# Retention's entry: the first chunk's small tiles in other places, PSUM banks laid out earlier, gate matmuls ahead of the first scores, odd feature tiles first

## The chip, the core and the metric

The kernel runs on one core of a Trainium2 chip. The metric is the device time of one execution in microseconds (us); for the kernel before it is the median of three runs. Engines are named as in the profile: PE is TensorE (matmuls; PEld its weight loads), DVE is VectorE, ACT is ScalarE, POOL is GpSimd, SP is SyncE, whose queue issues most of the transfers. Names of tiles in the profile are those of the program, with buffer numbers left out.

## The reference

One decoder block in float32 on a sequence of 1024 tokens with 1024 features. The input is normalised and modulated to `h`; from `h`, three kinds of mixing run side by side (chunkwise retention, dilated attention, and gates that merge them), then comes an MLP. What the edited place computes is the retention branch, for 4 heads with keys of 256, values of 512, in chunks of 128 tokens:

```python
def step(state, inp):
    qi, ki, vi = inp
    s = jnp.einsum('bhid,bhjd->bhij', qi, ki) * inner_decay[None]
    o = (jnp.einsum('bhij,bhje->bhie', s, vi)
         + jnp.einsum('bhid,bhde->bhie', qi, state) * q_decay[None, :, :, None])
    state = (state * chunk_decay[None, :, None, None]
             + jnp.einsum('bhjd,bhje->bhde', ki * k_decay[None, :, :, None], vi))
    return state, o
...
ret_out = (jax.nn.silu(rg) * ro) @ w_ret_out
```

Here `ro` is `o` normalised over the features of its head, and `rg` is a product of `h` with a gate weight, `h @ w_in` in the columns of the retention gate.

## The kernel before, in words

The instructions of all engines stand in the order in which the program writes them; nothing reorders them afterwards. A wait is put in by the tile pools: an instruction that writes a tile waits until whoever used that memory before is done, and with `reuse_waits="tile"` this is worked out for each old tile whose memory the new one covers.

Products are made in three matmuls (`mm3`, L197 to L205): each operand is split into a high and a low part, and low times high, high times low and high times high are summed in a PSUM bank. L201, L203 and L205 in the profile are those three, for every product that goes through `mm3`.

The stage ahead of the edited place is `values` (L1182). It makes the values of all heads and chunks in seven block products for each pair of heads, on sums `vc`, `va` and others in PSUM. `v_post` (L1152 to L1180) finishes each: VectorE adds a sum into `vr` (L1176), ScalarE takes its high part (L1177), VectorE its low part (L1178), and SP stores it to DRAM (`vd<-vr`, L1180). The last four such blocks are the last work of the stage. The tiles of that stage lie in `xpool` (L330). While the last product runs, GpSimd's queue loads the second halves of the even feature tiles of `h` back from DRAM (`hh<-h12d`, `hl<-h12d`, L1211 and L1212), since the even tiles (`hh[0]`, `hh[2]`, `hh[4]`, `hh[6]` and their low parts `hl`) held sums of blocks there. The odd ones hold `h` throughout.

At its end `values` closes `xpool` and opens the retention pool in the same memory (`open_ret`, L514: first `state`, then its high and low parts `stateh`, `statel`). Then it issues the loads for the second and third chunk (`fetch`, L583; the first chunk's values, and the queries and keys of the first two, were loaded earlier), then the first chunk's scores (`s_kt(0)`, L616), and then lays the PSUM banks out anew (`banks(False)`, L148): eight single banks before, and after it four single ones and two pairs, the pairs for the gates.

`s_kt` makes the scores `sT` of a chunk (L624, L626) and the transposed keys `kT` (L631) on TensorE. ScalarE copies the scores into `sm` (L635), VectorE adds the other part (L636) and multiplies by the decay (L637), ScalarE and VectorE split the result into `smh` and `sml` (L638, L639), and the keys, with their decay, into `kh` (L645) and `kl` (L646).

Then the retention loop runs over 4 heads and 8 chunks (`chunk`, L672). For the first chunk of all (`g == 0`) it issues four of the eight feature tiles of the gate product `rg` (six matmuls each, two halves of the tokens times three parts), then `kv` from `kh`, `kl` and the values (six matmuls), copies of `kv` into `state` on VectorE (L696), the modulation sum that rides along (L452), the next chunk's scores (`s_kt(1)`), and the output `o` from `smh`, `sml` and the values (three matmuls). In later chunks `kv` stands first, then two feature tiles of the gate product, then the next scores, `o`, and the other two feature tiles. A gate product spans two chunks: feature tiles 0 to 3 in the even chunk and 4 to 7 in the odd one, in that order.

Of the kernel before, what the change touches and what calls it, by code (L numbers as in the profile page):

```python
# [11 lines left out]
F32 = mybir.dt.float32  # L12
F32R = mybir.dt.float32r
# [4 lines left out]
P = 128  # L18
D = 1024
S = 1024  # L20
NK = D // P
H = 4
C = 128
# [111 lines left out]
def block_kernel(ctx, tc, io, stop=None, dbg=None):  # L135
# [61 lines left out]
    def mm3(outs, w, xs, first, last, skip=False):  # L197

        wh, wl = w
        for o, (xh, xl) in zip(outs, xs):  # L200
            nc.tensor.matmul(o, wl, xh, start=first, stop=False, skip_group_check=skip)  # L201
        for o, (xh, xl) in zip(outs, xs):
            nc.tensor.matmul(o, wh, xl, start=False, stop=False, skip_group_check=skip)  # L203
        for o, (xh, xl) in zip(outs, xs):
            nc.tensor.matmul(o, wh, xh, start=False, stop=last, skip_group_check=skip)  # L205

    def wk(w, k):

        return w[0][:, k * P:(k + 1) * P], w[1][:, k * P:(k + 1) * P]
# [112 lines left out]
    def halves(h, l):  # L322
        return [(h[:, :512], l[:, :512]), (h[:, 512:], l[:, 512:])]

    hx = [halves(hh[k], hl[k]) for k in range(NK)]
# [149 lines left out]
        nc.vector.scalar_tensor_tensor(hl[k], xt[k], mods[:, SH1 + k:SH1 + k + 1], fv(hh[k]),  # L475
                                       op0=ALU.add, op1=ALU.subtract)

    def proj_mm(ps, w, ks=range(NK)):
        outs = ps if isinstance(ps, list) else [ps[:, 0, :], ps[:, 1, :]]
        for k in ks:  # L480
            mm3(outs, wk(w, k), hx[k], k == 0, k == NK - 1)

    def proj_gen(ps, w):
        for k in range(NK):
# [27 lines left out]
    R = {}  # L512

    def open_ret():  # L514
        x_ctx.close()
        R["p"] = ret_ctx.enter_context(tc.tile_pool(name="ret", bufs=1, reuse_waits="tile"))
        R["state"] = R["p"].tile([P, 2, DV], F32, name="state")
        R["sh"] = R["p"].tile([P, 2, DV], F32R, name="stateh")
        R["sl"] = R["p"].tile([P, 2, DV], F32R, name="statel")

    def etile(name, dt=F32):
        return R["p"].tile([P, 1024], dt, tag="E", bufs=12, name=name)
# [55 lines left out]
    hd = {}  # L578
# [37 lines left out]
    def s_kt(i):  # L616

        p = R["p"]
        g = i
        h, c = divmod(g, NC)  # L620
        t = hd["j", g]
        ps = ps_s(f"sT{h}{c}")
        for i in range(2):
            nc.tensor.matmul(ps[:, :2 * C], t[:, 0, 2 + i, :], t[:, :, i, :], start=i == 0, stop=False,  # L624
                             skip_group_check=True)
            nc.tensor.matmul(ps[:, :C], t[:, 1, 2 + i, :], t[:, 0, i, :], start=False, stop=i == 1,  # L626
                             skip_group_check=True)
        pk = ps_s(f"kT{h}{c}", (P, 2, P)) if c < NC - 1 else None
        if pk is not None:
            for i in range(2):  # L630
                nc.tensor.transpose(pk[:, i, :], hd["qk", g][:, 2 + i], ident)  # L631
        sm = p.tile([P, C], F32, tag="sm", bufs=1, name=f"sm{h}{c}")
        smh = p.tile([P, C], F32R, tag="smh", bufs=2, name=f"smh{h}{c}")
        sml = p.tile([P, C], F32R, tag="sml", bufs=2, name=f"sml{h}{c}")
        nc.scalar.copy(sm, ps[:, :C])  # L635
        nc.vector.tensor_add(sm, sm, ps[:, C:2 * C])  # L636
        nc.vector.tensor_mul(sm, sm, decay[:, h * C:(h + 1) * C])  # L637
        nc.scalar.copy(smh, sm)  # L638
        nc.vector.tensor_sub(sml, sm, fv(smh))  # L639
        hd["s", g] = (smh, sml)  # L640
        if pk is not None:
            kd = ct[:, CS_KDEC + h:CS_KDEC + h + 1]
            kh = p.tile([P, 2, P], F32R, tag="kh", bufs=1, name=f"kh{h}{c}")
            kl = p.tile([P, 2, P], F32R, tag="kl", bufs=1, name=f"kl{h}{c}")
            nc.scalar.mul(kh, pk, kd)  # L645
            nc.vector.scalar_tensor_tensor(flat(kl), flat(pk), kd, fv(flat(kh)), op0=ALU.mult, op1=ALU.subtract)  # L646
            hd["k", g] = (kh, kl)
# [24 lines left out]
    def chunk(h, c, ahead, w=None):  # L672
        p = R["p"]
        g = NC * h + c
        if g + 3 < NG:
            fetch(g + 3)
        if c % 2 == 0:
            hd["rgw"] = w
            hd["rgp"] = ps_mm(f"rg{h}{c}")
        ks = range(4 * (c % 2), 4 * (c % 2) + 4)  # L680
        if g == 0:
            proj_mm(hd["rgp"], hd["rgw"], ks)
        vh, vl = hd["v", g][:, 0], hd["v", g][:, 1]
        st, sh, sl = R["state"], R["sh"], R["sl"]
        kvs = []
        if c < NC - 1:
            kh, kl = hd["k", g]
            for i in range(2):
                kv = ps_s(f"kv{h}{c}{i}")
                mm3([kv], (kh[:, i, :], kl[:, i, :]), [(vh, vl)], True, True)  # L690
                kvs.append(kv)
        if g > 0:
            proj_mm(hd["rgp"], hd["rgw"], ks[:2])
        for i, kv in enumerate(kvs):
            if c == 0:
                nc.vector.tensor_copy(st[:, i, :], kv)  # L696
            else:
                nc.vector.scalar_tensor_tensor(st[:, i, :], st[:, i, :], float(GAMMA[h] ** C), kv,
                                               op0=ALU.mult, op1=ALU.add)
        ahead(2)  # L700
        if g + 1 < NG:
            s_kt(g + 1)
        po = ps_s(f"o{h}{c}")
        if c > 0:
            t = hd["j", g]
            for i in range(2):
                mm3([po], (t[:, 0, i, :], t[:, 1, i, :]), [(sh[:, i, :], sl[:, i, :])], i == 0, False)
        mm3([po], hd["s", g], [(vh, vl)], c == 0, True)
        if c < NC - 1:
            for i in range(2):  # L710
                nc.scalar.copy(sh[:, i, :], st[:, i, :])
                nc.vector.tensor_sub(sl[:, i, :], st[:, i, :], fv(sh[:, i, :]))
        if g + 2 < NG:
            jit_qk(g + 2)
        if g > 0:
            on_T(*divmod(g - 1, NC))
        if g > 0:
            proj_mm(hd["rgp"], hd["rgw"], ks[2:])
        bn = p.tile([P, 6], F32, tag="bn", bufs=2, name=f"bn{h}{c}")
        ba = p.tile([P, 2], F32, tag="ba", bufs=2, name=f"ba{h}{c}")  # L720
        gr = p.tile([P, 1], F32, tag="gr", bufs=2, name=f"gr{h}{c}")
        nc.vector.bn_stats(bn, po)
        nc.vector.bn_aggr(ba, bn)
        nc.vector.tensor_scalar(gr, ba[:, 1:2], ct[:, CS_QD2 + h:CS_QD2 + h + 1], GN_EPS, op0=ALU.mult, op1=ALU.add)
        nc.gpsimd.tensor_tensor(gr, gr, mhalf[:, 0:1], op=ALU.pow)
        nc.vector.tensor_mul(gr, gr, ct[:, CS_QD + h:CS_QD + h + 1])
        on = p.tile([P, DV], F32, tag="on", bufs=1, name=f"onm{h}{c}")
        nc.vector.tensor_scalar(on, po, ba[:, 0:1], gr, op0=ALU.subtract, op1=ALU.mult)
        hd["o", h, c] = on
        if c % 2 == 1:  # L730
            hd["srg", h, c // 2] = etile(f"srg{h}{c // 2}")
            nc.scalar.activation(hd["srg", h, c // 2], flat(hd["rgp"]), AF.Silu)
        if h > 0 and c < 4:
            u_final(h - 1, (c,))
# [447 lines left out]
    def values(ahead):  # L1182
        last = len(VSEQ) - 1
        for j in range(2):
            v_low(0, j)
        for i, (hp, n) in enumerate(VSEQ):
            if i + 2 <= last:
                v_load(i + 2)
            for p in range(4):
                v_mm(i, p)  # L1190
                if V["post"]:
                    v_post(*V["post"].pop())
                V["post"].append((i, p))
                if p < 2 and i < last:
                    v_w(i + 1, p)
                    if p:
                        v_low(i + 1, 0)
                if p == 2 and i < last:
                    v_low(i + 1, 1)

                if i == last - 2 and p == 2:
                    fetch(0)
                if i == last - 2 and p == 3:
                    first["release"]()
                if i == last - 1 and p in (1, 2):
                    jit_qk(p - 1)
                if i == last - 1 and p == 3:
                    ahead(2)
                if i == last and p == 0:
                    for m in range(4):  # L1210
                        nc.gpsimd.dma_start(hh[2 * m][:, 512:], h12_d[m][:, 0])  # L1211
                        nc.gpsimd.dma_start(hl[2 * m][:, 512:], h12_d[m][:, 1])  # L1212
        v_post(*V["post"].pop())
        open_ret()
        for g in (1, 2):
            fetch(g)
        s_kt(0)
        banks(False)

    for kk in range(4):  # L1220
# [1349 lines left out]
```

## Time and profile before

| | us |
|---|---|
| median of three runs | 2232.41 |
| lowest, highest of them | 2231.76, 2233.54 |
| the profiled execution, its own time | 2231.9 |
| its span, first to last instruction | 2230.1 |
| ScalarE, VectorE, GpSimd busy in the span | 912.4, 1470.1, 155.1 |

The page gives each engine's busy time, the groups of instructions that cost most, and the chain of work that ended last, followed back from the last instruction. A row of the timeline has the start and the length in us, the engine, the line, the operation, the tiles written and read, their shapes and the count; in brackets stands the idle time of the engine before it and what ended it. SPq is the queue of SP, from which transfers are issued. A matmul's length in the profile overlaps the next one's, so the pitch from start to start tells its rate.

### The profile page before, as it was taken

Reading aid. Unit: us, or ns where it says so; the run is one execution under the profiler, and the core shown is the slowest. Engines: PE = TensorE matmul, PEld = TensorE weight load, DVE = VectorE, ACT = ScalarE, POOL = GpSimd, SP = SyncE. Lnnn points to the kernel's source line nnn. Section 1 sums busy time; section 2 is a strip of 40 time slices with the busy share of each in tenths; the row PEclk is TensorE's granted clock in tenths of the full one; section 3 lists DMA queues with packets and bytes.
Section 4 is the critical chain, followed back from the end, with each engine's and each line's share of the span. In section 5 each row is a group of like instructions: output and inputs, shape, how many; then the busy total and the mean of one; then the engine's idle time right before and its main releaser. Section 6 shows DMA issues by size and latency. Waiting matters only on the chain.

```text
span 2230.1 us, 27097 instructions
## 1 busy us (share of the span) xinstructions
PE 2168.7 (97%) x10082; PEld 1796.1 (81%) x10082; DVE 1470.1 (66%) x2303; ACT 912.4 (41%) x1671; POOL 155.1 (7%) x176
## 2 busy tenths in 40 slices
PE   7999999999989999999999999999999999999998
PEld 5888888878868888888788788888778888788887
DVE  6756777754448778865555654676866665787845
ACT  4532233223324444544634633524444445533412
POOL 0100111000012112200000000002000000000003
PEclk9999999999999999999999999999999999999999
DMA  9869999634675556559723265654234444745322
GB/s 383 220 208 299 294 296 277 189 131 174 224 255 170 181 178 203 185 175 238 224 73 96 92 219 187 237 180 159 69 135 147 155 156 165 261 141 170 123 85 76
DMA packets 157602, 414.15 MB, mean 186 GB/s; under 512 B 27222, under 2 KB 55133, under 8 KB 153054
## 3 DMA queue, kind: packets, MB, share of 16 engines
q1 hardware_dynamic: 149598, 364.19, 46.5%
q0 software_dynamic: 7872, 48.24, 9.5%
q8 instruction: 79, 1.29, 0.2%
q14 instruction: 53, 0.43, 0.1%
HBM read 321.51 MB, written 156.13 MB: 214 GB/s over the span
## 4 chain that ended last, share of the span: by engine, by line
PE 86%; DVE 6%; DMA 4%; ACT 3%; issue 1%; POOL 0%; SPq 0%; POOLq 0%; DVEq 0%; ACTq 0%
PE qap L203 5%; PE qap L201 5%; PE qap L205 5%; PE fp L201 4%; PE fp L203 4%; PE fp L205 4%; PE rg L201 3%; PE rg L203 3%; PE rg L205 3%; PE f2a L203 2%; PE f2a L205 2%; PE f2a L201 2%; PE ak L201 2%; PE ak L203 2%; PE ak L205 2%; PE va L203 1%
## 5 line engine op out<-in xcount | busy, mean ns | idle before, releaser
L201 PE MATMUL qap<-hh,qaw 128*128 128x512 f32 x216 | 84.1, 390 | 0.4 <-DVE qat L285 0.4
L205 PE MATMUL qap<-hh,qaw 128*128 128x512 f32 x216 | 84.0, 389 | 0.0
L203 PE MATMUL qap<-hl,qaw 128*128 128x512 f32 x216 | 84.0, 389 | 0.0
L613 POOL TENSOR_TENSOR j<-qk,j 128x512 fp32r<-128x512 f32 x32 | 43.3, 1353 | 462.2 <-ACT j L612 462.2
L2029 ACT ACTIVATE a<-a 128x512 f32<-128x512 f32 x48 | 30.3, 632 | 79.5 <-DVE a L2028 79.5
L1926 POOL TENSOR_TENSOR accnf<-accnf,sqnf 128x256 f32<-128x256 f32 (+1 forms) x18 | 16.6, 921 | 620.2 <-ACT sqnf L1925 620.2
L1383 ACT ACTIVATE P<-P,ng 128x128 f32<-128x128 f32 (+1 forms) x96 | 41.9, 438 | 39.0 <-DVE ng L1380 39.0
L258 DVE TENSOR_TENSOR fw<-w1r,fw 128x512 fp32r<-128x512 f32 x48 | 32.9, 687 | 36.2 <-ACT fw L248 36.2
L2215 ACT CAST w2h<-w2s 128x512 fp32r<-128x512 f32 x36 | 22.3, 621 | 77.6 <-DVE w2s L2253 73.6
L635 ACT COPY sm<-sT 128x128 f32<-128x128 f32 x32 | 8.5, 265 | 111.0 <-PE sT L626 103.8
L201 PE MATMUL fp<-h2h,fw 128*128 128x512 f32 x128 | 50.0, 390 | 0.0
L203 PE MATMUL fp<-h2l,fw 128*128 128x512 f32 x128 | 49.8, 389 | 0.0
L205 PE MATMUL fp<-h2h,fw 128*128 128x512 f32 x128 | 49.8, 389 | 0.0
L201 PE MATMUL roa<-rh,rwl 128*128 128x512 f32 x128 | 49.8, 389 | 0.0
L203 PE MATMUL roa<-rl,rwh 128*128 128x512 f32 x128 | 49.8, 389 | 0.0
L205 PE MATMUL roa<-rh,rwh 128*128 128x512 f32 x128 | 49.8, 389 | 0.0
L1764 DVE TENSOR_TENSOR rwl<-rwl,rwh 128x1024 fp32r<-128x1024 f32 x25 | 30.2, 1220 | 29.1 <-ACT rwh L1794 29.1
L1926 POOL TENSOR_TENSOR accn<-accn,sqn 128x512 f32<-128x512 f32 x12 | 15.5, 1293 | 478.2 <-ACT sqn L1925 478.2
L201 PEld LDWEIGHTS qap<-hh,qaw 128*128 128x128 f32 x216 | 40.5, 188 | 9.2 <-DVE qat L285 0.8
L203 PEld LDWEIGHTS qap<-hl,qaw 128*128 128x128 f32 x216 | 40.5, 188 | 8.4
L205 PEld LDWEIGHTS qap<-hh,qaw 128*128 128x128 f32 x216 | 40.5, 188 | 8.4
L258 DVE TENSOR_TENSOR qaw<-wa,qaw 128x512 fp32r<-128x512 f32 x54 | 37.0, 686 | 10.0 <-ACT qaw L248 10.0
(3063 smaller groups left out, 7188.1 us busy)
## 6 DMA issues: line engine op xcount, KB each, us to landing
v<-vd SPq DMA_DIRECT2D x32, 512.0 KB, 4.8
raw<-in_w_ada_dram SPq DMA_DIRECT2D x32, 512.0 KB, 5.1
w1r<-in_w_ff_dram SPq DMA_DIRECT2D x32, 512.0 KB, 4.8
vd<-vo SPq DMA_DIRECT2D x24, 512.0 KB, 4.4
yt<-y POOLq DMA_DIRECT2D x6, 2048.0 KB, 16.5
xsd<-as SPq DMA_DIRECT2D x24, 512.0 KB, 2.7
w2r<-in_w_ff2s_dram SPq DMA_DIRECT2D x24, 512.0 KB, 7.3
em<-in_w_ada_dram SPq DMA_DIRECT2D x16, 512.0 KB, 10.2
```

Source lines behind the costliest of these rows:

```text
L201: nc.tensor.matmul(o, wl, xh, start=first, stop=False, skip_group_check=skip)
L203: nc.tensor.matmul(o, wh, xl, start=False, stop=False, skip_group_check=skip)
L205: nc.tensor.matmul(o, wh, xh, start=False, stop=last, skip_group_check=skip)
L258: nc.vector.tensor_sub(t[:, 512:], src, fv(t[:, :512]))
L613: nc.gpsimd.tensor_sub(t[:, 1], src, fv(t[:, 0]))
L635: nc.scalar.copy(sm, ps[:, :C])
L1383: nc.scalar.activation(v, v, AF.Exp, bias=ng[:, blk:blk + 1], accum_out=st[:, g, blk, 2 + a:3 + a])
L1764: nc.vector.tensor_sub(lo, fv(lo), fv(hi))
L1926: (nc.vector if f == 7 else nc.gpsimd).tensor_add(G["acc", key], G["acc", key], sq)
L2029: nc.scalar.activation(o, o, AF.Relu)
L2215: nc.scalar.copy(hi, src)
```

## The change

The order of work on TensorE at retention's entry, the memory of five small tiles of the first chunk, and the order of the feature tiles in all gate products of the retention loop change; what is computed does not.

```diff
-    def proj_mm(ps, w, ks=range(NK)):
+    def proj_mm(ps, w, ks=range(NK), order=range(NK)):
         outs = ps if isinstance(ps, list) else [ps[:, 0, :], ps[:, 1, :]]
-        for k in ks:
-            mm3(outs, wk(w, k), hx[k], k == 0, k == NK - 1)
+        for i in ks:
+            mm3(outs, wk(w, order[i]), hx[order[i]], i == 0, i == NK - 1)
...
     def open_ret():
         x_ctx.close()
         R["p"] = ret_ctx.enter_context(tc.tile_pool(name="ret", bufs=1, reuse_waits="tile"))
+        for n in R_SMALL:
+            R[n] = r_small(n, "00")
         R["state"] = R["p"].tile([P, 2, DV], F32, name="state")
...
+    R_SMALL = {"sm": ([P, C], F32, 1), "kh": ([P, 2, P], F32R, 1), "kl": ([P, 2, P], F32R, 1), "smh": ([P, C], F32R, 2),
+               "sml": ([P, C], F32R, 2)}
+
+    def r_small(n, name):
+
+        if n in R:
+            return R.pop(n)
+        shape, dt, bufs = R_SMALL[n]
+        return R["p"].tile(shape, dt, tag=n, bufs=bufs, name=n + name)
...
-        sm = p.tile([P, C], F32, tag="sm", bufs=1, name=f"sm{h}{c}")
-        smh = p.tile([P, C], F32R, tag="smh", bufs=2, name=f"smh{h}{c}")
-        sml = p.tile([P, C], F32R, tag="sml", bufs=2, name=f"sml{h}{c}")
+        sm, smh, sml = (r_small(n, f"{h}{c}") for n in ("sm", "smh", "sml"))
...
-            kh = p.tile([P, 2, P], F32R, tag="kh", bufs=1, name=f"kh{h}{c}")
-            kl = p.tile([P, 2, P], F32R, tag="kl", bufs=1, name=f"kl{h}{c}")
+            kh, kl = (r_small(n, f"{h}{c}") for n in ("kh", "kl"))
...
         if g == 0:
-            proj_mm(hd["rgp"], hd["rgw"], ks)
+            proj_mm(hd["rgp"], hd["rgw"], ks[:2], (1, 3, 5, 7, 0, 2, 4, 6))
+            s_kt(0)
+            proj_mm(hd["rgp"], hd["rgw"], ks[2:], (1, 3, 5, 7, 0, 2, 4, 6))
...
         if g > 0:
-            proj_mm(hd["rgp"], hd["rgw"], ks[:2])
+            proj_mm(hd["rgp"], hd["rgw"], ks[:2], (1, 3, 5, 7, 0, 2, 4, 6))
...
         if g > 0:
-            proj_mm(hd["rgp"], hd["rgw"], ks[2:])
+            proj_mm(hd["rgp"], hd["rgw"], ks[2:], (1, 3, 5, 7, 0, 2, 4, 6))
...
         for g in (1, 2):
             fetch(g)
-        s_kt(0)
         banks(False)
```

The five tiles are taken from the retention pool as soon as it is opened, ahead of `state`, and the first call of `s_kt` uses them. The first chunk's scores are issued inside `chunk`, between the first two and the next two feature tiles of the gate product, and so after the banks are laid out anew.

## The prediction

> **What bounds the kernel now.** I read the page's busy table and its chain first, then who waited for whom on TensorE around the edited place, then that place instruction by instruction on each engine, the granted clock in stretches, and last the transfers.
>
> ```profile
> span 2230.1 us, 27097 instructions
> PE 2168.7 (97%) x10082; PEld 1796.1 (81%) x10082; DVE 1470.1 (66%) x2303; ACT 912.4 (41%) x1671; POOL 155.1 (7%) x176
> PE 86%; DVE 6%; DMA 4%; ACT 3%; issue 1%; POOL 0%; SPq 0%; POOLq 0%; DVEq 0%; ACTq 0%
> PE rg L201 <- DVE kl L646: 10.1, 1, 10.1
> PE kv L201 <- DVE kl L646: 2.5, 1, 2.5
> SPq L600 <- DMA vd<-vr: 2.5, 1, 2.5
> ```
>
> TensorE is busy 97% of the span and carries 86% of the chain, so only time in which it stands still or runs slowly is to be had. The last three rows are from the waits between 600 and 700 us: on TensorE there are two, one of 10.1 us before the first gate matmul (`rg`) and one of 2.5 us before the second chunk's `kv`. Both end with `kl`. The third row belongs to the load queue and is used below.
>
> The chain of waits, in order of time, tells what made the first `kl` late:
>
> ```profile
> 647.42 0.70 DVE vr L1176
> 648.79 0.70 DVE vr L1178
> 649.51 6.35 DMA vd<-vr
> 655.97 0.27 ACT sm L635
> 656.26 0.30 DVE sm L636
> 657.21 0.38 ACT kh L645
> 657.62 0.49 DVE kl L646
> 658.15 1.22 PE rg L201 x2
> ```
>
> The last value block is stored (`vd<-vr`, issued at 649.51, landed 6.35 us later), and only then is the score block copied into `sm`. From there it is 2.18 us to the gate matmuls (655.97 to 658.15). `sm` has no use for that store; it stands where the store's source stood. The gates have no use for `kl` either; their banks were last read by it.
>
> TensorE's own rows, and the one of ScalarE that I need:
>
> ```profile
> 647.23 0.28 PE L624 MATMUL sT<-j 128*128 128x256 f32 x1
> 647.63 0.40 PE L631 MATMUL kT<-ct,qk 128*128 128x128 f32 x2
> 658.15 1.22 PE L201 MATMUL rg<-hh,raw_4651l 128*128 128x512 f32 x2 [10.13 <-DVE kl L646]
> 665.23 0.39 PE L201 MATMUL kv<-v,kl 128*128 128x512 f32 x1
> 666.59 0.28 PE L624 MATMUL sT<-j 128*128 128x256 f32 x1
> 667.15 0.48 PE L201 MATMUL o<-v,sml 128*128 128x512 f32 x1
> 667.70 0.40 PE L205 MATMUL o<-v,smh 128*128 128x512 f32 x1
> 670.62 0.50 PE L201 MATMUL kv<-v,kl 128*128 128x512 f32 x1 [2.52 <-DVE kl L646]
> 667.20 0.27 ACT L635 COPY sm<-sT 128x128 f32<-128x128 f32 x1 [9.61 <-PE sT L626]
> ```
>
> Between the end of the values (647.23) and the second chunk's `kv` (670.62) lie 23.39 us. The clock in stretches of 3.41 us:
>
> ```profile
> 491.00:494.41 3.41, 1.93 (x9) 1.00 0.38 154
> 647.70:651.11 3.41, 0.33 (x4) 1.00 1.10 397
> 651.11:654.53 3.42, 0.00 (x0) 0.50 1.08 391
> 657.94:661.35 3.41, 3.20 (x8) 0.50 0.69 246
> 661.35:664.77 3.42, 3.42 (x16) 1.00 0.02 5
> 668.18:671.59 3.41, 0.97 (x4) 1.00 0.57 147
> 671.59:675.01 3.42, 3.42 (x9) 0.50 0.68 236
> ```
>
> Columns: stretch, length, TensorE busy, granted clock, transfer share, GB/s. The clock follows the stretch before: 0.33 or 0.97 us busy out of 3.41 is followed by half clock, 3.20 by full clock. So the first stall costs 10.13 us and also slows the gates behind it: 24 of them take 7.08 us (658.15 to 665.23), where six full-clock matmuls of the same width take 1.36 (`kv`, 665.23 to 666.59), or 0.227 each, 5.45 for 24. That is 1.63 more. The second stall's half stretch costs half of 3.41, 1.71.
>
> **The change part by part.**
>
> *Other places for the small tiles.* `sm`, `smh`, `sml`, `kh`, `kl` of the first chunk are now the first tiles of the retention pool. In the built program the first copy into `sm` waits for TensorE alone. This takes the 6.35 us store out of the chain; no instruction is added. The price is that `state` and its halves move onto stored tiles: the first `state` copy now waits for the first of the four `vr` stores, `stateh` and `statel` for the second.
>
> *Banks laid out sooner, gates first.* The gates now take banks that held value sums, the last of which they need was read long before 647; `sT` needs the last value sum read, which is over at 647.42 + 0.70 = 648.12. The moved step issues six matmuls on TensorE, three operations on ScalarE and four on VectorE, and no transfer; it passes 12 gate matmuls on TensorE, while on ScalarE and VectorE it stays next in line after the values. Nothing is removed: the same count of matmuls runs.
>
> *Odd feature tiles first.* The even tiles' second halves are reloaded on GpSimd's queue:
>
> ```profile
> 635.01 0.61 POOL L1211 DMA_DIRECT2D hh<-h12d  x1 [1.43 <-PE va L205]
> 641.89 0.53 POOL L1212 DMA_DIRECT2D hl<-h12d  x1 [3.06 <-issue]
> DMA to landing us min/median/max: 6.6/10.7/15.1
> hl<-h12d POOLq DMA_DIRECT2D x1, 256.0 KB, 13.4
> 635.44 1.23 DVE L192 TENSOR_TENSOR raw_4651l<-raw,raw_4651h 128x1024 fp32r<-128x1024 f32 x1 [0.19 <-ACT raw_4651h L191]
> ```
>
> The third row is for the `hh` reloads, the fourth for the last `hl`. From the first issue, 635.01 + 10.7 is 645.7 and + 15.1 is 650.1, the last is 641.89 + 13.4 = 655.3. Even tiles at 647 could therefore have waited up to some 3 us; odd ones have nothing to wait for, and their weights are ready at 636.67. The even tiles come up in the second chunk, after 659, so the cover holds by 4 us.
>
> *The new order, added up from 647.23.* 12 gates at 0.227: 649.95. `sT` and `kT` take 0.56 (666.59 to 667.15): 650.51. 12 gates: 653.23. Meanwhile `sm` is copied 0.61 after `sT` began (667.20 less 666.59), at 650.56, and 2.18 later, at 652.74, `kl` lets `kv` go: 0.49 before TensorE comes to it, so no wait. Six `kv`: 654.59. Second `sT`, `kT`: 655.15. `o`, three matmuls, 0.95 (667.15 to 667.70 and 0.40 more): 656.10. The second chunk's `kv` came 4.03 after its `sT` (666.59 to 670.62), behind the state copies, a modulation sum and the score chain on VectorE, all of which stand in the same order; so it comes at 654.59 + 4.03 = 658.62, with the same stall of 2.52. Queued behind that wait are all gates of the chunk.
>
> 670.62 − 658.62 = **12.0 us**: 10.13 of stall, 1.63 of slow gates and 0.24 of overlap at the ends. TensorE sets the pace from there on, so I carry it to the end.
>
> *The transfers now needed earlier.*
>
> ```profile
> 641.36 8.47 SPq L1180 DMA_DIRECT2D vd<-vr  x4
> 652.41 0.32 SPq L600 DMA_DIRECT2D v<-vd  x1
> vd<-vr SPq DMA_DIRECT2D x4, 512.0 KB, 7.3
> v<-vd SPq DMA_DIRECT2D x3, 512.0 KB, 5.2
> ```
>
> The second chunk's `v` was held 2.5 us by the second `vr` store (the queue's row above), which thus landed near 652.4; now it waits for earlier stores only and can be issued at 649.9. The stores that `state` waits for are landed by 652.4 too, and `state` is first written at about 654.1. Not shown is how long a load takes behind the last store. Bounds: 5.2 (loads) gives 655.1; 13.4 (the last `hl`) gives 663.3, 4.7 us after it is needed. I take 7.3, the stores of the same queue in the same traffic: 657.2, 1.4 before 658.62. The load of the fourth chunk's `qk` waits for the last store (655.9) and holds the queue until then; what stands behind it is needed a chunk later or more.
>
> *The clock at the second stall.* 2.52 us of idle time leave 0.89 busy if they fall into one stretch of 3.41. 0.97 was followed by half clock, 1.93 (the row at 491) was not. Where the stretches fall I cannot know; over all placements the idle part is long enough in 0.31 (by the bound 0.97) to 0.87 (by 1.93) of the cases. I take 0.6, near the middle, and price the half stretch at 1.71 as before. [...]
>
> *Sum.* The profiled execution took 2231.9 us (span 2230.1); 2231.9 − 12.0 = 2219.9, with the half stretch still there. Its own time lies 0.5 under the median of the runs, 2232.41.
>
> **The rivals.**
>
> *No half stretch at the second stall,* since its idle time falls across two stretches: 2219.9 − 1.71 = 2218.2. For it: the row at 491; against: the row at 668.18. [...]
>
> *`v` or the score chain late.* `kl` has 0.49 us of slack and `v` 1.4. A load of 13.4 us adds 4.7: 2224.6. For it: transfers are saturated until the last store lands. Against: the load is next in the queue and was 5.2.
>
> *The change doesn't do what it says:* if something still ties `sm` to the last store, `kl` frees `kv` at 658.15 as before instead of 653.23, with 24 gates done meanwhile: 4.92 of new stall and about 1.7 of half clock, 2226.5. Against: the new wait list.
>
> *Slower:* the same load of `v`, on the same queue as four stores of 512 KB and beside the reloads, becomes the bound. Every us after 658.6 is a us on the path; from 12.0 on, that is from a landing after 670.6 or 20.7 us after issue, the kernel is slower than before. The longest landing in these rows is 15.1, on the other queue, so this needs contention that no row shows: at 25 us, 4.3 more than before, 2236.2.
>
> **How the numbers follow.** Forecast 0.55, no half stretch 0.32, something late 0.06, still tied 0.04, slower 0.03. Predicted: 2219.9. Low end: 2218.2 less the 0.65 that the fastest run shown lies under the median, 2217.5. High end: 2219.9 plus the 1.6 from the profiled execution to the slowest run shown, plus part of the late cases, 2223.0. What a measurement of this kernel can tell from no change is about 0.2%, 4.5 us: faster means under 2227.9. The first four cases are all faster at their prices; of the late and the tied case I give 0.02 to a result within 4.5 us. Faster 0.95, same 0.02, slower 0.03.
>
> **What would show it.** Right: gate matmuls begin within 0.3 us of the last value matmul and run at about 0.227 from the first; full clock between 651 and 661; `sm` copied near 650.6; one wait on `kl` of about 2.5 us before the second `kv`, at about 658.6. Wrong: a wait before the first `kv` (score chain late), `v` named as what ended the second stall, a wait before `state` that ends with `vd<-vr`, or gate matmuls of even tiles that wait for `hh<-h12d`. If the entry shows 12 us gained and the total does not, a later stage has taken it back, and the forecast's last step is wrong.

## The result and the profile after

The changed kernel took 2222.98 us (median of four runs, 2220.01 to 2224.21) beside 2232.12 for the kernel before (2231.76 to 2233.54): a ratio of 0.9956 with a 95% interval of 0.9939 to 0.9973. Two later measurements of the same kernel gave 2220.64 and 2219.87 (below). All 14 runs have a median of 2220.2; the forecast was 2219.9. Against the kernel before run beside them, the three medians are 9.1, 11.7 and 12.3 lower, where 12.0 was forecast.

The page of the kernel after, its head, its busy table and its chain by engine:

```profile
span 2220.8 us, 27106 instructions
...
PE 2168.2 (98%) x10082; PEld 1796.1 (81%) x10082; DVE 1469.8 (66%) x2303; ACT 912.6 (41%) x1671; POOL 155.1 (7%) x176
...
PE 87%; DVE 6%; ACT 3%; issue 1%; DMA 1%; POOL 0%; SPq 0%; POOLq 0%; DVEq 0%; ACTq 0%
```

All waits of TensorE between 600 and 700 us (engine, line, tile, what it waited for: us in total, times, longest):

```profile
PE kv L201 <- DVE kl L655: 2.5, 1, 2.5
```

Against the page before: TensorE's busy time is the same (2168.7 there), and the span is 9.3 shorter. The nine more instructions are semaphore operations; no matmul, copy or transfer is new. The chain's DMA share has gone from 4% to 1%, but little of that is the edit's: the store was 6.35 us, 0.3% of the span, and the chain of before also ran through the loads at the start, some 50 us, where the chain of after does not. Of the two waits at the entry, the one of 10.1 us before `rg` is gone and the one of 2.5 us before the second `kv` remains.

Rows of the timeline of the kernel after, TensorE's, then ScalarE's and the load queue's (start, length, engine, line, operation, tiles, shapes; in brackets the idle time before it):

```profile
646.73 0.61 PE L201 MATMUL rg<-hh,raw_4651l 128*128 128x512 f32 x2
...
649.45 0.28 PE L636 MATMUL sT<-j 128*128 128x256 f32 x1
...
652.86 0.39 PE L201 MATMUL kv<-v,kl 128*128 128x512 f32 x1
...
654.22 0.28 PE L636 MATMUL sT<-j 128*128 128x256 f32 x1
...
658.25 0.79 PE L201 MATMUL kv<-v,kl 128*128 128x512 f32 x1 [2.52 <-DVE kl L655]
```

```profile
650.05 0.27 ACT L645 COPY sm<-sT 128x128 f32<-128x128 f32 x1 [1.78 <-PE sT L638]
```

```profile
649.45 0.41 SPq L612 DMA_DIRECT2D v<-vd  x1
```

The values end 0.50 earlier in this execution than in the one of before (646.73 against 647.23), so 0.50 comes off every time of the prediction. The gates start with no gap in front of them. The scores start 2.72 later (12 gates at 0.227 are 2.72). `kv` starts 6.13 after the gates (forecast 653.23 − 647.23 = 6.00) and waits for nothing. The second `kv` comes at 658.25, where 658.62 − 0.50 = 658.12 was forecast, behind the same stall of 2.52. ScalarE's copy into `sm` now waits for the score matmul instead of the store, and the load of `v` is issued at 649.45 and named in no wait.

The clock in stretches, kernel after (stretch, length, TensorE busy with matmuls, granted clock, transfer share, GB/s):

```profile
647.59:651.00 3.41, 3.41 (x19) 1.00 1.12 401
651.00:654.42 3.42, 3.42 (x18) 1.00 1.06 410
654.42:657.83 3.41, 1.31 (x9) 1.00 1.02 350
657.83:661.25 3.42, 3.00 (x7) 0.50 1.00 340
...
1125.45:1128.87 3.42, 2.57 (x23) 1.00 0.00 0
1128.87:1132.29 3.42, 3.42 (x11) 0.50 0.00 0
```

The first gates run at full clock, as forecast, and the second stall is followed by one stretch of half clock, as forecast. The last two rows lie 470 us later, in the attention: a stretch of half clock that the kernel before didn't have there.

Where the time went is best read from the start of the same matmul in both traces. The table gives its start in the kernel named less its start in the kernel before, in us, near five times of the kernel before. The entry's gain is the difference of the first two columns.

| kernel | 640 | 690 | 1075 | 1150 | 2200 | entry's gain |
|---|---|---|---|---|---|---|
| the change | −0.50 | −12.56 | −12.58 | −9.78 | −9.43 | 12.06 |
| the change again | +1.57 | −11.89 | −11.80 | −11.31 | −11.00 | 13.46 |
| the change, third time | +0.94 | −12.55 | −12.43 | −12.14 | −11.97 | 13.49 |
| places alone | +0.95 | −7.43 | −7.44 | −7.42 | −8.32 | 8.38 |
| order alone | −0.97 | −8.35 | −8.28 | −7.50 | −9.11 | 7.38 |
| even tiles first | −0.99 | −13.15 | −13.15 | −10.37 | −10.74 | 12.16 |
| scores first | +0.72 | −10.08 | −10.12 | −9.68 | −10.10 | 10.80 |
| two gate tiles ahead of the second `kv` | −0.22 | −13.70 | −13.66 | −12.05 | −12.60 | 13.48 |
| later read-back | −0.82 | −12.94 | −12.98 | −11.08 | −10.80 | 12.12 |
| sum behind `onm` | −1.00 | −14.38 | −14.30 | −14.33 | −14.40 | 13.38 |
| sum in the idle place | +1.47 | −13.04 | −12.90 | −10.97 | −11.59 | 14.51 |

The first profile gained 12.06 at the entry, of 12.0 forecast, and gave back 2.80 between 1075 and 1150: 0.95 before the attention gates near 1080, 0.2 by 1095, and 1.65 near the stretch of half clock at 1128.87.

### The profile page after: what moved, and what is told of

It is laid out like the page before. It is cut to its first block, busy times and chain, and to the rows that moved or that the text cites. A ratio compares the mean times of both kernels' runs of the same rounds, so it can differ in the third digit from the quotient of the medians.

```text
span 2220.8 us, 27106 instructions
## 1 busy us (share of the span) xinstructions
PE 2168.2 (98%) x10082; PEld 1796.1 (81%) x10082; DVE 1469.8 (66%) x2303; ACT 912.6 (41%) x1671; POOL 155.1 (7%) x176
## 4 chain that ended last, share of the span: by engine, by line
PE 87%; DVE 6%; ACT 3%; issue 1%; DMA 1%; POOL 0%; SPq 0%; POOLq 0%; DVEq 0%; ACTq 0%
PE qap L203 5%; PE qap L201 5%; PE qap L205 5%; PE fp L201 4%; PE fp L203 4%; PE fp L205 4%; PE rg L201 3%; PE rg L203 3%; PE rg L205 3%; PE f2a L203 2%; PE f2a L205 2%; PE f2a L201 2%; PE ak L201 2%; PE ak L203 2%; PE ak L205 2%; PE va L203 1%
## 5 line engine op out<-in xcount | busy, mean ns | idle before, releaser
L258 DVE TENSOR_TENSOR qaw<-wa,qaw 128x512 fp32r<-128x512 f32 x54 | 36.9, 686 | 12.1 <-ACT qaw L248 12.1
```

The source lines that it names most:

```text
L258: nc.vector.tensor_sub(t[:, 512:], src, fv(t[:, :512]))
```

## The experiments

Edits are shown against the changed kernel. Ratios are to the kernel before, run on the same chip, with 95% intervals.

### The change measured again, twice

> The changed kernel again, in more runs. Its first profile gained 12.1 us at the entry (from the last value matmul to the second chunk's kv) and lost some 2.7 us later: one half-clock stretch near 1129 us (1.7) and a late gate weight near 1050 us (0.9). Theory A, both come and go with the placement of the clock's stretches and with the timing of GpSimd's DRAM sums: median 2221 to 2223, runs spread over 3 to 4 us, and in each run the time falls by about 1.7 us for each 3.4 us less of half clock. Theory B, the loss belongs to the change: the same two places in this profile, median 2222.5 to 2223.5, little spread.

> The changed kernel once more, beside the run with the sum in the idle place, on the same chip. If the first measurement's 2223.0 was the run-to-run place of half-clock stretches: 2219.5 to 2222, as the second measurement was, and a second stall of 2.5 us in the profile. If the change has two settled levels: 2222.5 to 2224.

2220.64 (2219.14 to 2221.15), ratio 0.9946 [0.9934, 0.9959], and 2219.87 (2217.72 to 2220.21), ratio 0.9941 [0.9927, 0.9954]. The second measurement lies 0.4 under the range given for it, with runs 2.0 apart instead of 3 to 4; the loss near 1129 did not come back, which is against the theory that it belongs to the change. Waits of TensorE at the entry are the same single 2.5 us as in the first profile. Its half stretch is missing in both; the clock table of the third profile shows why:

```profile
491.11:494.52 3.41, 1.34 (x7) 1.00 0.54 216
494.52:497.93 3.41, 3.41 (x9) 0.50 1.00 292
...
654.94:658.36 3.42, 2.23 (x13) 1.00 1.02 381
658.36:661.77 3.41, 2.08 (x9) 1.00 1.03 325
661.77:665.18 3.41, 3.41 (x20) 1.00 0.93 333
```

The same 2.52 us of idle time falls into two stretches here, 1.19 and 1.33, and neither is followed by half clock; in the second profile it is 1.51 and 1.01; in the first 2.10 of it fell into one. The entry's gain is 13.46 and 13.49 without the half stretch and 12.06 with it. Both of these profiles have another half stretch, after an older stall near 492, ahead of the edit (first two rows); it stands in the +0.94 and +1.57 of the table.

Seven profiles of this study have the second stall at its 2.5 us behind a full-clock stretch: the three of the change, and the ones with the places alone, even tiles first, scores first and the later read-back. Four of them have the half stretch and three not. The first measurement's spread has the same cause as far as its numbers tell: its fastest run, 2220.01, had a mean granted clock of 0.997, the other three (2222.60 to 2224.21) 0.995. A deficit of 0.002 over 2220 us is 4.4 us, give or take the rounding of two figures; the difference is 2.6 to 4.2.

### The places alone

```diff
-            proj_mm(hd["rgp"], hd["rgw"], ks[:2], (1, 3, 5, 7, 0, 2, 4, 6))
-            s_kt(0)
-            proj_mm(hd["rgp"], hd["rgw"], ks[2:], (1, 3, 5, 7, 0, 2, 4, 6))
+            proj_mm(hd["rgp"], hd["rgw"], ks)
...
+        s_kt(0)
         banks(False)
```

The order of the later chunks' tiles is the one of before as well.

> The small tiles in their new places alone; scores ahead of the banks and of the gates, even tiles in order, as before. Theory A (two ties: sm to the last store through memory, the gates to kl through the banks): sm is copied near 648.8 instead of 655.97, the gates begin near 651.4 instead of 658.15, still behind kl, or up to 2 us later behind the reload of even tiles; 6.7 us less stall and 0 to 1.6 us less half clock, so 2224 to 2226. Theory B (the order of the work does it all): 2232, as before.

2225.01 (2223.66 to 2229.05), ratio 0.9973 [0.9963, 0.9984]. Waits of TensorE, 600 to 700 us:

```profile
PE rg L201 <- DVE kl L655: 3.3, 1, 3.3
PE kv L201 <- DVE kl L655: 2.5, 1, 2.5
```

The wait of 10.1 us has become 3.3: the store is out of the chain, but the gates still come after `kl`, through their banks. So the store was worth 6.8 of the first stall and the banks the other 3.3. A half stretch (652.76 to 656.17) still follows the 3.3 us.

### The order alone

```diff
-        for n in R_SMALL:
-            R[n] = r_small(n, "00")
...
-        sm, smh, sml = (r_small(n, f"{h}{c}") for n in ("sm", "smh", "sml"))
+        sm = p.tile([P, C], F32, tag="sm", bufs=1, name=f"sm{h}{c}")
```

and the same for `smh`, `sml`, `kh` and `kl`: the five tiles lie where they lay before; gates first, banks sooner and odd tiles first stay.

> Gates first, banks sooner, odd tiles first; the small tiles in their old places. Theory A: sm still waits for the last store (655.9), kl frees the first chunk's kv at 658.1 instead of 652.9; 24 gates are done meanwhile, so 5 us of new stall and 1 to 2 us of half clock: 2227 to 2230. Theory B (the order does it all): 2222 to 2223, as the whole change.

2225.99 (2223.40 to 2231.56), ratio 0.9976 [0.9967, 0.9986]. Waits of TensorE, 600 to 700 us, then ScalarE's first copy in the timeline:

```profile
PE kv L201 <- DVE kl L656: 5.9, 2, 4.5
```

```profile
654.87 0.27 ACT L645 COPY sm<-sT 128x128 f32<-128x128 f32 x1 [7.07 <-DMA vd<-vr]
```

The copy into `sm` still waits for the store, now 7.07 us, and the wait reaches TensorE at the first `kv` as 4.5 us; the other 1.4 stand before the second `kv`. Half clock then lasted two stretches, 6.83 us from 656.04. This is the rival "still tied" built on purpose: I had priced it at 4.92 of new stall, about 1.7 of half clock, 2226.5 in all; the median lies 0.5 under that and 1.0 under the range given ahead of the run. The profile is of the lowest of the eleven runs, which spread over 8 us; what the higher ones lost beyond it isn't shown. Each part alone gains some 7 to 8 at the entry and both together 12.1 to 13.5: the two chains run side by side, and each alone leaves the other's remainder.

### Even feature tiles first

The whole change with the tuple `(1, 3, 5, 7, 0, 2, 4, 6)` taken out at all four places.

> The whole change but for the odd tiles first: the gates take tiles 0 to 3 in order. Theory A: the gates wait for the reload of the even tiles, which land 10 to 15 us after their issue at 635 to 638: a stall of 0 to 4 us ahead of or among the first 12 gates, ended by hh<-h12d or hl<-h12d, part of it with half clock after it: 2223 to 2228. Theory B, the reloads are there in time: no such wait, 2222 to 2223.

2221.22 (2216.50 to 2223.08), ratio 0.9946 [0.9933, 0.9958]. No matmul waited for a reload of `hh` or `hl`; the only wait at the entry is the 2.5 us, and the entry's gain is 12.16 with a half stretch (the change with one: 12.06). The order of the tiles does nothing that shows here.

### Scores first, banks laid out ahead of them

```diff
-            proj_mm(hd["rgp"], hd["rgw"], ks[:2], (1, 3, 5, 7, 0, 2, 4, 6))
             s_kt(0)
-            proj_mm(hd["rgp"], hd["rgw"], ks[2:], (1, 3, 5, 7, 0, 2, 4, 6))
+            proj_mm(hd["rgp"], hd["rgw"], ks, (1, 3, 5, 7, 0, 2, 4, 6))
```

> The whole change, but the first scores stay ahead of all gates; the banks are still laid out before them. Theory A (what ties the gates to kl is the banks, so gates need not stand first): the gates follow the transposed keys at once, sm is copied near 649, kl is long done before kv; a wait of 0.5 to 1.5 us ahead of sT until the last value sum is read; 2221 to 2223, within 1.5 us of the whole change. Theory B (only the gates' place ahead of the scores hides the chain): a stall of 2 us or more before the gates or kv, 2224 or more.

2220.84 (2218.99 to 2222.43), ratio 0.9945 [0.9932, 0.9959].

```profile
PE kv L201 <- DVE kl L655: 2.5, 1, 2.5
PE sT L636 <- DVE vr L1186: 0.9, 1, 0.9
```

With the banks laid out sooner the gates need not stand first: what it costs to have the scores in front is 0.9 us, the wait for the last value sum to be read. The entry gained 10.80, 1.26 less than the change's 12.06; 0.9 of it is this wait, about 0.2 is the half stretch behind the second stall, which is busy for all of its 3.41 us here and for 3.00 in the change, and the rest I can't place. The total cannot be told from the change's.

### Two gate tiles ahead of the second `kv`

```diff
+        if g == 1:
+            proj_mm(hd["rgp"], hd["rgw"], ks[:2], (1, 3, 5, 7, 0, 2, 4, 6))
         if c < NC - 1:
...
-        if g > 0:
+        if g > 1:
             proj_mm(hd["rgp"], hd["rgw"], ks[:2], (1, 3, 5, 7, 0, 2, 4, 6))
```

> The whole change, and in the second chunk too the first two gate tiles ahead of kv. Theory A (the second stall is the score chain's time with nothing else to do on TensorE): 12 gates take 2.7 us where 2.52 stood idle; no wait of over 0.5 us on TensorE between 640 and 700, no half-clock stretch there; 2.5 to 4.2 us less than the whole change: 2217 to 2218.5. Theory B (the stall moves, to v or to the state, or comes back a chunk later): a wait of 1 to 2.5 us at kv or at the next o, 2220 to 2222.

2219.75 (2218.11 to 2222.66), ratio 0.9943 [0.9930, 0.9955].

```profile
PE kT L643 <- DVE onm L741: 1.0, 1, 1.0
PE sT L636 <- POOL j L625: 0.8, 1, 0.8
PE o L201 <- DVE state L711: 0.2, 1, 0.2
```

The gates fill the stall and TensorE then waits a step later: of the 2.52 us, 2.0 come back as three smaller waits, two that end with VectorE's work (1.0 and 0.2) and one with GpSimd's (0.8). No stretch held enough idle time to be followed by half clock, so the entry's gain is that of the change without a half stretch, 13.48 against 13.46 and 13.49.

### The sum that stands ahead of the score chain

VectorE's order in the first chunk is state copies, modulation sum, score chain. Two runs move the sum: behind that chunk's `onm`, and into the time in which VectorE is idle ahead of the state copies.

```diff
             s_kt(0)
+            ahead(2)
...
-        ahead(2)
+        if g > 0:
+            ahead(2)
```

This is the second of them; the first has its `if g == 0: ahead(2)` behind `onm` instead.

> The whole change, and in the first chunk the modulation sum on VectorE (1.22 us in the profile after, with 0.08 and 0.16 behind it) stands behind that chunk's onm, instead of ahead of the second chunk's score chain. Nothing is left out. Theory A (the second stall is VectorE's order: state copies, then the sum, then the score chain up to kl): sm's addition starts at once behind the state copies, 1.3 us earlier, the second kv's wait on kl is 1.2 (2.52 less 1.3) instead of 2.5, and with 1.2 us of idle time no stretch of half clock follows at the entry: about 1.3 us less than the change wherever that had no half stretch, 3.0 where it had one, 2217.5 to 2220. Entry gain against before 14.7 to 14.9. Theory B (the sum only moves, as the stall did when two gate tiles were put ahead): onm or what follows it (kT, the next score) waits for VectorE up to 1.3 us a step later, entry gain at most 13.5, 2219.5 to 2222.

> The whole change, and in the first chunk the modulation sum on VectorE stands right behind the first score chain, ahead of the state copies, where the profile after has VectorE idle for 1.55 us (between kl, ended 652.20, and the first state copy, 653.74). Nothing is left out. Theory A (the second stall is VectorE's order, and the sum, 1.33 us from its start to the next operation, fits into that idle time): the second kv's wait on kl is 1.2 to 1.3 us, as when the sum stood behind onm, and the 1.1 us wait of o for state, seen there, is not there; no stretch of half clock at the entry, entry gain against before 14.7, 1.3 more than the best of the change. Time 2217 to 2219.5. Theory B (the sum does not fit, because its load or its work comes late, and the state copies are pushed back): the second stall stays above 2 us or a wait of o for state comes up; entry gain at most 13.5, 2219.5 to 2222.

Behind `onm`: 2219.04 (2217.52 to 2225.49), ratio 0.9946 [0.9933, 0.9960]. In the idle place: 2220.20 (2218.64 to 2221.75), ratio 0.9945 [0.9932, 0.9957]. Waits of TensorE with the sum behind `onm`:

```profile
PE kv L201 <- DVE kl L655: 1.3, 1, 1.3
PE o L201 <- DVE state L709: 1.1, 1, 1.1
```

And with the sum in the idle place, the only wait, then rows of VectorE's timeline:

```profile
PE kv L201 <- DVE kl L655: 1.3, 1, 1.3
```

```profile
654.07 1.22 DVE L452 SCALAR_TENSOR_TENSOR raw<-raw,cb 128x1024 f32<-128x1024 f32 x1
...
655.70 1.37 DVE L708 COPY state<-kv 128x512 f32<-128x512 f32 x2 [0.21 <-PE kv L205]
657.09 0.29 DVE L646 TENSOR_TENSOR sm<-sm,sT 128x128 f32<-128x128 f32 x1
```

Both times the second stall falls from 2.52 to 1.3, by the sum's 1.3. Behind `onm` the sum is in the way of the next state update, and 1.1 us come back; in the idle place nothing comes back, since VectorE is still 0.21 us idle before the state copies. The entry's gain is 14.51, 1.0 more than the best of the change. So 1.3 of the second stall's 2.52 is VectorE's order, not a latency that has to be there; the other 1.3 wasn't tried. The total doesn't show that 1.0 and lies 0.7 over the range given for it: this profile has half stretches at 495.80 and 1127.27, some 1.5 us each, and the one with the sum behind `onm` has neither; that one has the shortest span of all the profiles, 2215.9.

### A later read-back, at the place that gave time back

In the first profile the wait of the attention gate near 1066 was 1.7 us (before: 0.8), and ScalarE's weight part ahead of it had waited 0.84 for its load, which stood in the queue behind the read-back of a 16 KB statistics tile. The store of that tile and its read-back in the load queue's timeline, in the kernel before and then after:

```profile
1046.76 0.33 SPq L1441 DMA_DIRECT2D std<-st  x1
...
1053.48 0.38 SPq L1442 DMA_DIRECT2D stn<-std  x1
```

```profile
1034.18 0.33 SPq L1451 DMA_DIRECT2D std<-st  x1
...
1044.82 0.38 SPq L1452 DMA_DIRECT2D stn<-std  x1
```

The read-back waits for the store: 6.7 us from issue to issue before, 10.6 after, though the store is issued 12.6 earlier. The run moves the read-back behind the next loads of the queue:

```diff
-        nc.sync.dma_start(A["stn"][:, g], natural(d, 0, 4))
+        dst = A["stn"][:, g]
+        A["late"] = lambda: nc.sync.dma_start(dst, natural(d, 0, 4))
...
                 weave(gen, NK, scores_gen(pair, *last), len(SB[last[0]]), lag=2)
+                if "late" in A:
+                    A.pop("late")()
```

> The whole change, and in the attention stage the read-back of the score statistics stands behind the next gate weights' loads in the queue. Theory A (the late gate weight near 1050 comes from the read-back, which holds the queue while the statistics' store lands in 10 us beside a DRAM sum): no wait of ScalarE for that load in this profile and the loads issued some 9 us sooner; TensorE's wait before the gate at 1068 is 0.8 or less, and the entry's 12 us reach the end but for half-clock stretches: 2219 to 2220.5. Theory B (that wait is the softmax chain's own, whatever the loads do): TensorE still waits 0.8 to 2 us there, 2220.5 to 2222.

2219.18 (2218.46 to 2221.14), ratio 0.9940 [0.9928, 0.9953]. The weight no longer waited, but the gate did, 2.8 us, since the read-back itself was now late:

```profile
1061.54 0.17 DVE L1465 TENSOR_TENSOR mx<-mx,stn 128x16 f32<-128x16 f32 x1 [5.18 <-DMA stn<-std]
```

My edit traded one wait for a longer one, so it doesn't show what the queue's order was worth. Nor is it the whole cause: in the change's two later profiles the store took as long (10.9 and 11.3 us from its issue to the read-back's), and the gate waited 0.8 and 1.1; with even tiles first it waited 2.0, and the weight part ahead of it had waited for no load. That wait varies between executions, from 0.8 to 2.0 in the unedited place, and why stays open.

No variant is shown to beat the change: the intervals of the two halves (places alone, order alone) lie above those of its second and third measurement, and all the others overlap with them.

## Why the prediction was right, point by point

- **The store's tie and the banks.** Right, with both parts shown: 6.8 us of the first stall came through `sm`'s place (places alone); the other 3.3 went once the banks were laid out sooner, with the scores still first and 0.9 of another wait in their place.
- **The new order, added up.** Right to 0.13 us over eleven and a half: the second `kv` was forecast 11.39 after the values' end and came at 11.52.
- **`kl`'s slack, `v`, and the state's ties.** Right: no wait for any of them in any profile of the change. How much later `v` could have come wasn't tried.
- **Odd tiles first.** I let even tiles wait "up to some 3 us". That was the end of a bound worked out from landings (median 10.7, longest 15.1); none of it occurred. It entered no term of the sum.
- **Full clock for the gates.** Right; 1.63 of the 12.0 rests on it.
- **Half clock at the second stall.** I gave it 0.6 by where the stretches fall; it came in four profiles of seven. The most idle time in one stretch was 2.03, 2.08, 2.10 and 2.52 us in these four, and 1.83, 1.51 and 1.33 in the three without; from these I estimate the chance for 2.52 us at 0.55 to 0.67. That my 0.6 lies there is in part luck: the row at 491.00, from which I took the upper bound, lies off the steps in which this trace shows the clock change. Half clock in the kernel before begins at 651.11, lasts 10.24 us, three steps of 3.4133, and begins again at 671.59 and 1640.97, 6 and 290 such steps after 651.11. Counted back, the stretches begin at 490.68 and 494.09, and hold more busy time than 1.93:

```profile
490.68:494.09 3.41, 2.25 (x10) 1.00 0.38 154
494.09:497.51 3.42, 2.51 (x11) 1.00 0.84 265
```

The price was mis-sized: 1.71 is half of a whole stretch, but the stretch begins while TensorE still stands. The row at 657.83 has 3.00 busy of 3.42, and half of 3.00 is 1.5; the entry's gain with and without it differs by 1.4.

- **Carried to the end.** This is the step that the first measurement missed, as the last sentence on what would show it had put it: the entry gained 12.06 and the span 9.3. Its median, 2222.98, lies just under the upper end of the range, 2223.0, and that it stayed inside is luck: what the profiled run (2222.6) holds beyond 2219.9 isn't the late load or score chain that this end allowed for, but half clock near 1129 and a longer wait of the attention gate. A second and a third measurement ended 11.0 and 12.0 ahead near 2200. No stage takes a fixed part of the gain back: from 690 to 2200 the three profiles lose 3.1, 0.9 and 0.6, and the one with the sum behind `onm` nothing. What differs is where stalls of 0.9 to 2.5 us fall, at 492, 657 and 1126, whether half clock follows, and how long the gate waits. The forecast had a chance for this at one of those places and held the others as in the profile of before.

## What to carry to other kernels

When a stall ends with an engine that had long been idle, look for what shares its memory: a new tile on the source of a store inherits that store (6.8 us here), and a bank inherits its last reader (3.3 us), and each may hide behind the other, so undo both before judging either. A stall that is filled with other work can come back a step later, as 2.0 of 2.52 us did here; what removed 1.3 us of it was to move that much VectorE work into VectorE's own idle time. On a kernel with many stalls like the one of 2.5 us here, which half clock followed in four profiles of seven, carry a gain to the end with a spread of two or three half stretches, and measure twice.

## What the runs showed of the hardware that I had not expected

TensorE's busy time alone does not tell whether half clock follows a stretch. A stretch with 1.58 busy in the places alone was followed by full clock, and one with 1.75 in the order alone by half clock:

```profile
663.00:666.41 3.41, 1.58 (x7) 1.00 0.76 210
666.41:669.82 3.41, 3.41 (x20) 1.00 0.47 174
```

```profile
1591.30:1594.71 3.41, 1.75 (x6) 1.00 0.00 0
1594.71:1598.12 3.41, 3.41 (x9) 0.50 0.02 5
```

And 2.57 busy with 23 matmuls of 128 columns, the row at 1125.45 in the profile after, was followed by half clock. Those narrow ones start 0.11 us apart, where 512 columns take 0.227. What sets these rows apart was not shown: no run was built to test it.
